# Small input features token by token behind the first receptance block, with later softmax pieces, in a hybrid decoder layer on one Trainium2 core

## The chip, the cores and the metric

One core of one Trainium2 chip runs the whole layer. The metric is the device time of one execution in microseconds; the time of a kernel is the median of its runs. TensorE (PE) multiplies, VectorE (DVE) and ScalarE (ACT) do the element-wise work, GpSimd (POOL) very little, and SyncE (SP) issues nearly all DMAs.

## The reference, cut to what matters

A decoder layer of width 2048 over 256 tokens: two parallel token mixers (mLSTM and RWKV-7), cross-attention into 256 memory tokens, and a gated feed-forward. The change touches the narrow columns of the input projection and the softmax of the cross-attention.

```python
proj = h @ w_in                      # h = rms_norm(x)
q, k, v, o, ir, fr = split_cols(mlstm_p, MLSTM_COLS)      # ir, fr: 4 gate columns each
rp = rwkv_p + (shift_right(rwkv_p, 1) - rwkv_p) * mu      # mix with the token before
r, kr, vr, wl, al, gl = split_cols(rp, RWKV_COLS)         # wl, al 64 columns each, gl 160
...
scores = jnp.einsum('bshd,bmhd->bhsm', q, k).astype(jnp.float32) * (XATTN_HEAD_DIM ** -0.5)
p = jax.nn.softmax(scores, axis=-1).astype(v.dtype)
o = jnp.einsum('bhsm,bmhd->bshd', p, v).reshape(B, S, XATTN_WIDTH)
```

`wl`, `al`, `gl`, `ir` and `fr` are 64 + 64 + 160 + 4 + 4 = 296 columns, the small features.

## The kernel before, in words

Every large product is done with three float32r products: activations and weights are each split into a high and a low part (`hh`, `hl` and `wh`, `wl`), and high x high, low x high and high x low are summed in PSUM. The work is a list of blocks, one for 512 output columns as a rule (`block`, run in order by `run`). A block reads its weights in chunks of two k-tiles of 128 rows. `Feed` brings a chunk by a DMA from SP, casts it to `wh` on ACT (L375) and subtracts `wl` on DVE (L396), three chunks ahead of PE in four buffers, so a cast waits until PE has left the chunk four places before. A block is feature-major (`fm`: the weights are stationary, 256 tokens move, the output has features on partitions) or token-major (`tm`: the activations are stationary, the weight columns move, the output has tokens on partitions). Its sums stand in two of four PSUM banks, so a block's first matmul waits until the banks of the block before the last are evacuated.

The rest, evacuations and all other mathematics, is written as Python generators. The planner `Spread` places one piece of them (up to the next `yield`) at a time between the matmuls: at every half chunk (`half`, twice a chunk) DVE gets 640 and ACT 820 units of credit, capped at 1200, and a piece of the first bulk task or of the first two back tasks runs while both credits are positive; chain tasks run every so many halves. `need` runs a task to its end at once. The order on every engine is thus fixed when the program is written.

The order of the blocks at the front: the small features (`sm`, the 296 columns padded to 384, feature-major), receptance 0 and 1 (`r_evac`), keys, values, and so on. While the first block runs, the input is split (`x_split`), and its squares are summed for the norm (`st0`). `sm_evac` ends the statistic (`st0.finish`: a fold on DVE, a column matmul, the root on POOL, a row matmul, a copy), multiplies the sums by it, mixes each token with the one before (`shiftmix`, ACT then DVE), and adds two tasks: `gates` (mLSTM gates) and `sm_rest` (the low-rank decay and rate, products `zwa`). The keys' groups (`k_group`), `inverses` and the recurrence `rwkv` wait for these, and its end feeds `hb_split` (products `zg`), whose output `hb` a later block needs (`need_hb`).

In the cross-attention the blocks are keys (`xk`), a quarter of the values (`xv`), queries (`xq_`), the rest of the values. Beside them the residual (`Residual.run`) produces the queries' input and the squares of its norm, whose column (`early_column`, tile `st` from `stx`) the softmax needs. `stagger` runs the four heads of `softmax` in steps of one half: scores `xsc`, exponentials `spr`, turned rows `xpT`. The attention product `xo` follows the values.

Of the kernel before, what the change touches and what calls it, by code (L numbers as in the profile page):

```python
# [15 lines left out]
P = 128  # L16
D = 2048
S = 256
# [127 lines left out]
def _layer(ctx, tc, nc, d, dbg):  # L146
# [96 lines left out]
    class Stat:  # L243
# [65 lines left out]
        def early_column(self):  # L309
            self.fold()  # L310
            yield
            yield
            self.column()
# [16 lines left out]
    class Feed:  # L330
        def __init__(self, order):
            self.kind = [k for k, s in order]
            self.src = [s for k, s in order]
            self.raw, self.st, self.nd, self.ns, self.nl = {}, {}, 0, 0, 0

            self.sm = [big(f"wsm{i}", [P, 4, 2, 384]) for i in range(2)]

# [21 lines left out]
        def staged(self, name, r, i):  # L359


            k, c = r.shape[1:]
            up = i - len(self.src) + 384
            o = 0
            if self.kind[i] == "fm":
                o = 16 if i % (16 if up >= 0 else 4) else 24
            w = wp.tile([P, 1024 + 128], F32R, tag=name, bufs=4, name=name)
            return w[:, o:o + k * c].rearrange("p (k c) -> p k c", k=k)

# [39 lines left out]
    def tm_products(o, t, c, wx, first, last):  # L409
        wh, wl, xh, xl = wx  # L410
        t = slice(t // P * P, t // P * P + P)
        c = slice(c, c + 512)
# [19 lines left out]
    def run():  # L432
# [8 lines left out]
        for b, c0, c1 in order:  # L441
            if c0 == 0:
                if len(pend) >= 2 and b["pool"] is acc:
                    side.need(pend[-2])
                if b["before"]:
                    b["before"]()
                n = (b["cols"] // P + 1) // 2 if b["kind"] == "fm" else 2 * (b["cols"] // 512)
                b["banks"], b["k"] = [], 0
                for _ in range(n):
                    if b["pool"] is acc:  # L450
                        if len(ring) >= 4:
                            side.need(ring[-4]["task"])
                        ring.append(b)
                    b["banks"].append(b["pool"](b["kind"], [P, 2, S] if b["kind"] == "fm" or b is xv else None))
                if b["bankwise"]:
# [8 lines left out]
            for ci, s in enumerate(srcs):  # L464
# [9 lines left out]
                for kj in range(s.shape[1]):  # L474
# [19 lines left out]
                    else:  # L494
                        for g, o in enumerate(banks):
                            tm_products(o, g * P * 512 // b["cols"], g * 512 % b["cols"], (wh[:, kj], wl[:, kj], xh, xl),
                                        first, last)
# [46 lines left out]
            if end:  # L544
                b["task"] = side.add(b["evac"](banks))
                if b is xq_:
                    side.need(b["task"])
                pend.append(b["task"])
# [18 lines left out]

    def pre_sm(ci, feed):
        if ci == 0:
# [13 lines left out]

    def pre_r0(ci, feed):
        if ci == 0:
# [17 lines left out]

    def sm_evac(ps):
        dve.tensor_scalar(om, pcol("mu", 0, 27), -1.0, 1.0, op0=ALU.mult, op1=ALU.add)
# [4 lines left out]
        yield from st0.finish(3)  # L610
        pr = PR()
        dve.tensor_mul(pr, ps[0], bc(st0.rb, 2))
        wa, gl = C("wa", "m0"), T2("gl")
# [3 lines left out]
        yield  # L617
        pr = PR()
        dve.tensor_mul(pr[:, 0], ps[1][:, 0], st0.rb)
        shiftmix(gl1, pr[:, 0], 26, slice(0, 32))  # L620
        R = [T2("rows") for _ in range(4)]
        M["rows"] = R
        tasks["gates"] = side.add(gates(), chain=1)
        act.copy(R[0][0:4, 0], pr[32:36, 0])
        act.copy(R[0][0:4, 1], pr[64:68, 0])
        act.activation(wa[0:64], wa[0:64], AF.Tanh)
# [940 lines left out]
    def stagger(gens):  # L1567
# [16 lines left out]
    def softmax(h):  # L1584
# [43 lines left out]

    block("fm", W("w_xk", 0), mxs, kx_evac, before=start_res1)
    xv = block("tm", W("w_xv", 0), mxs, vx_evac, tail=2)  # L1630
# [237 lines left out]
def prepare(i):  # L1868
# [32 lines left out]
    o["con"] = constants()  # L1901
    z = lambda n: np.zeros((D, n), np.float32)
    smw = np.concatenate([w[:, 6152:6440], w[:, 3072:3076], z(28), w[:, 3076:3080], z(60)], 1)
    o["w_sm"] = np.ascontiguousarray(smw.reshape(8, 2, P, 384).transpose(0, 2, 1, 3))
    ga, gb = w[:, 6440:8488], w[:, 8488:10536]
# [29 lines left out]
```

## Time and profile before

| | |
|---|---|
| median of 3 runs | 1896.22 us (1896.04 to 1896.8) |
| profiled execution | 1896.41 us, span 1894.2 us |
| PE busy | 1878.4 us (99% of the span) |
| DVE busy | 1297.0 us (68%) |
| ACT busy | 1012.7 us (53%) |
| mean granted TensorE clock | 0.999 |
| weight DMAs of the small features | 7 of 384 KB and 2 of 192 KB |

Busy time of PE counts overlapping matmuls once; what one of them costs is seen from the starts of its neighbours. A row of a timeline gives start, duration, engine, source line, operation, output and inputs, shape, count, and in brackets the idle time ahead of it with what ended it. In the view of waits a row gives total time, number and longest.

### The profile page before, as it was taken

The numbers are of one execution on the slowest core, as the hardware profiler recorded it, in microseconds if no ns is written. First come the engines' busy times: TensorE is split into PE (matmuls) and PEld (weight loads), VectorE is DVE, ScalarE is ACT, GpSimd is POOL, SyncE is SP. The second block draws the span as 40 slices with busy tenths as digits, with TensorE's granted clock in tenths as the row PEclk, the third lists the DMA queues.
The fourth block names the chain that finished last, engine by engine and source line by source line (L and its number), as shares of the span: only waits on it lengthen the run. The fifth ranks groups of instructions, "written<-read, shape, count | busy, mean of one in ns | idle before, by whom it ended". The sixth has DMA issues, their size and how long they took to land.

```text
span 1894.2 us, 36440 instructions
## 1 busy us (share of the span) xinstructions
PE 1878.4 (99%) x15066; PEld 1788.5 (94%) x15066; DVE 1297.0 (68%) x1834; ACT 1012.7 (53%) x1467; POOL 22.4 (1%) x39
## 2 busy tenths in 40 slices
PE   9999999999999999899999999999999999999998
PEld 9999988999999999899999999999999998888886
DVE  7878787565675857677767766667766675556555
ACT  7676435555454645566555444455444455455554
POOL 0100000000000000000000000000000000000000
PEclk9999999999999999999999999999999999999999
DMA  7655554444556755455555555555566556556554
GB/s 267 184 168 182 183 157 149 136 153 157 167 171 210 268 201 179 134 163 186 193 189 190 191 198 193 197 190 190 191 198 196 195 190 219 192 190 198 191 191 142
DMA packets 98199, 352.20 MB, mean 186 GB/s; under 512 B 11057, under 2 KB 11825, under 8 KB 97649
## 3 DMA queue, kind: packets, MB, share of 16 engines
q1 hardware_dynamic: 97168, 348.86, 56.1%
q8 instruction: 118, 1.93, 0.4%
q10 hardware_dynamic: 864, 1.01, 0.2%
q14 instruction: 49, 0.39, 0.1%
HBM read 347.73 MB, written 2.10 MB: 185 GB/s over the span
## 4 chain that ended last, share of the span: by engine, by line
PE 95%; DVE 2%; ACT 1%; issue 1%; DMA 0%; ACTq 0%; DVEq 0%
PE fm L181 67%; PE tm L181 24%; DVE wl L396 1%; PE gram L181 0%; PE Y L181 0%; ACT wh L375 0%; DVE rows L66 0%; PE lv L181 0%; PE num L181 0%; DMA wsm<-in_w_sm_dram 0%; ACT spr L66 0%; PE X L181 0%; PE gramA L181 0%; PE U L181 0%; DVE ql L66 0%
## 5 line engine op out<-in xcount | busy, mean ns | idle before, releaser
L396 DVE TENSOR_TENSOR wl<-raw,wh 128x1024 fp32r<-128x1024 f32 x640 | 780.1, 1224 | 437.9 <-ACT wh L375 435.1
L375 ACT CAST wh<-raw 128x1024 fp32r<-128x1024 f32 x640 | 668.4, 1049 | 530.5 <-PE fm L181 408.6
L181 PE MATMUL fm<-fh,wh 128*128 128x256 f32 x2048 | 567.4, 277 | 1.4 <-ACT fh L66 1.4
L181 PE MATMUL fm<-fh,wl 128*128 128x256 f32 x2048 | 566.5, 277 | 0.0
L181 PE MATMUL fm<-fl,wh 128*128 128x256 f32 x2048 | 566.4, 277 | 0.0
L181 PEld LDWEIGHTS fm<-fh,wh 128*128 128x128 f32 x2048 | 384.9, 188 | 1.5 <-ACT fh L66 1.5
L181 PEld LDWEIGHTS fm<-fh,wl 128*128 128x128 f32 x2048 | 384.9, 188 | 0.0
L181 PEld LDWEIGHTS fm<-fl,wh 128*128 128x128 f32 x2048 | 384.9, 188 | 0.0
L181 PE MATMUL tm<-wh,as 128*128 128x512 f32 x1024 | 315.7, 390 | 0.8 <-DVE as L66 0.8
L181 PE MATMUL fm<-hh,wh 128*128 128x256 f32 x1072 | 301.9, 282 | 0.0
L181 PE MATMUL fm<-hh,wl 128*128 128x256 f32 x1072 | 299.7, 280 | 0.5 <-DVE wl L396 0.5
L181 PE MATMUL fm<-hl,wh 128*128 128x256 f32 x1072 | 299.3, 279 | 0.0
L181 PEld LDWEIGHTS tm<-wh,as 128*128 128x128 f32 x1024 | 192.2, 188 | 41.1 <-DVE as L66 1.1
L181 PEld LDWEIGHTS fm<-hh,wh 128*128 128x128 f32 x1072 | 202.8, 189 | 1.6 <-ACT hh L66 0.3
L181 PEld LDWEIGHTS fm<-hh,wl 128*128 128x128 f32 x1072 | 202.3, 189 | 1.2 <-DVE wl L396 0.9
L181 PEld LDWEIGHTS fm<-hl,wh 128*128 128x128 f32 x1072 | 202.3, 189 | 0.1
L181 PE MATMUL tm<-wl,as 128*128 128x512 f32 x512 | 199.3, 389 | 0.0
L181 PEld LDWEIGHTS tm<-wl,as 128*128 128x128 f32 x512 | 96.1, 188 | 19.9
L66 ACT CAST as<-ac 128x256 fp32r<-128x256 f32 x128 | 45.6, 405 | 110.8 <-PE tm L181 110.8
L66 DVE TENSOR_TENSOR as<-ac,as 128x256 fp32r<-128x256 f32 x128 | 48.6, 422 | 61.6 <-ACT as L66 61.6
L181 PE MATMUL fm<-mgh,wh 128*128 128x256 f32 x256 | 71.4, 279 | 0.0
L181 PE MATMUL fm<-mgl,wh 128*128 128x256 f32 x256 | 71.2, 278 | 0.0
(376 smaller groups left out, 2168.4 us busy)
## 6 DMA issues: line engine op xcount, KB each, us to landing
raw<-in_w_fu_dram SPq DMA_DIRECT2D x256, 512.0 KB, 4.3
raw<-in_w_in_dram SPq DMA_DIRECT2D x160, 512.0 KB, 3.7
raw<-in_w_fd_dram SPq DMA_DIRECT2D x128, 512.0 KB, 4.3
raw<-in_w_br_dram SPq DMA_DIRECT2D x32, 512.0 KB, 4.2
raw<-in_w_mo_dram SPq DMA_DIRECT2D x32, 512.0 KB, 4.3
raw<-in_w_xk_dram SPq DMA_DIRECT2D x8, 512.0 KB, 4.3
raw<-in_w_xv_dram SPq DMA_DIRECT2D x8, 512.0 KB, 3.7
raw<-in_w_xq_dram SPq DMA_DIRECT2D x8, 512.0 KB, 3.8
```

What stands on the lines that cost most here:

```text
L66: return f(out, *a, **k)
L181: pe.matmul(out, lhsT, rhs, start=start, stop=stop, skip_group_check=True)
L375: nc.scalar.copy(wh, r)
L396: nc.vector.tensor_sub(wl, r, self.st[self.nl][0])
```

## The change

The first receptance block becomes the first block of the list, and its evacuation now begins with the statistic (`statistic`). The small features follow as a token-major block of 296 columns without padding. Their evacuation scales each token by its own factor on ACT, from PSUM to two tiles, waits three halves, turns them with six transposes on PE, and then mixes from PSUM as before. Second receptance block and the rest follow as they were. The keys of the cross-attention are evacuated as soon as their block ends; the statistic column waits five halves instead of two behind its fold; a softmax head is started at every second half, with one half more between scores and exponentials and two more between exponentials and turning. The first eight chunks go into tiles of 512 columns, and the staged weights' rows are padded to a multiple of 64.

```diff
         def early_column(self):
             self.fold()
-            yield
-            yield
+            for _ in range(5):
+                yield
             self.column()
...
-            self.sm = [big(f"wsm{i}", [P, 4, 2, 384]) for i in range(2)]
+            self.sm = [big(f"w0{i}", [P, 4, 2, 512]) for i in range(2)]
...
-            return w[:, o:o + k * c].rearrange("p (k c) -> p k c", k=k)
+            e = -(-c // 64) * 64
+            return w[:, o:o + k * e].rearrange("p (k c) -> p k c", k=k)[:, :, 0:c]
...
-                if b is xq_:
+                if b is xq_ or b is xk:
                     side.need(b["task"])
...
-    def sm_evac(ps):
+    def statistic():
         dve.tensor_scalar(om, pcol("mu", 0, 27), -1.0, 1.0, op0=ALU.mult, op1=ALU.add)
         dve.tensor_scalar(oka, pcol("ka", 0, 8), -1.0, 1.0, op0=ALU.mult, op1=ALU.add)
         for c in (6, 7):
             st0.add(xq[c])
             yield
         yield from st0.finish(3)
-        pr = PR()
-        dve.tensor_mul(pr, ps[0], bc(st0.rb, 2))
+
+    def sm_evac(ps):
+        s1, s2 = T2("smw"), C("smr", "mt1", [P, 2, 96])
+        pool.memset(s2, 0.0)
+        for t in range(2):
+            r = st0.rc[:, t:t + 1]
+            act.activation(s1[:, t], ps[t][:, 0:256], AF.Copy, scale=r)
+            act.activation(s2[:, t, 0:36], ps[t][:, 256:292], AF.Copy, scale=r)
+            act.activation(s2[:, t, 64:68], ps[t][:, 292:296], AF.Copy, scale=r)
+        for _ in range(3):
+            yield
+        pr, p2 = aux("smT", [P, 2, S]), aux("smT", [P, S])
+        for j in range(2):
+            for t in range(2):
+                pe.transpose(pr[:, j, t * P:(t + 1) * P], s1[:, t, j * P:(j + 1) * P], ident)
+        for t in range(2):
+            pe.transpose(p2[0:96, t * P:(t + 1) * P], s2[:, t], ident)
         wa, gl = C("wa", "m0"), T2("gl")
         gl0, gl1 = gl[:, 0], gl[:, 1]
         shiftmix(wa, pr[:, 0], 24)
         shiftmix(gl0, pr[:, 1], 25)
         yield
-        pr = PR()
-        dve.tensor_mul(pr[:, 0], ps[1][:, 0], st0.rb)
-        shiftmix(gl1, pr[:, 0], 26, slice(0, 32))
+        shiftmix(gl1, p2, 26, slice(0, 32))
...
             if hf == 0:
+                yield from statistic()
                 M["rr"] = U("rr")
...
-    block("fm", [d["w_sm"][c] for c in range(8)], xs0, sm_evac, cols=384, pre=pre_sm)
-    for hf in range(2):
-        block("fm", W("w_in", hf), xs0, r_evac(hf), pre=pre_r0 if hf == 0 else None)
+    block("fm", W("w_in", 0), xs0, r_evac(0), pre=pre_r0)
+    block("tm", [d["w_sm"][c] for c in range(8)], xs0, sm_evac, cols=296, pre=pre_sm)
+    block("fm", W("w_in", 1), xs0, r_evac(1))
...
+        n = 1
         while live or left:
-            if left:
+            if left and n % 2 == 0:
                 live.append(left.pop(0))
+            n += 1
...
         dve.tensor_reduce(mx, q, axis=AX.X, op=ALU.max)
         yield
+        yield
...
-        yield
+        for _ in range(3):
+            yield
         q = aux("xpT", [P, 2, S])
```

More of the change, by code (lines that the diff above doesn't have):

```diff
@@ L411, in tm_products @@
         t = slice(t // P * P, t // P * P + P)
-        c = slice(c, c + 512)
+        c = slice(c, c + o.shape[1])
         mm(o, xh[:, t], wh[:, c], start=first, stop=False)
@@ L446, in run @@
                     b["before"]()
-                n = (b["cols"] // P + 1) // 2 if b["kind"] == "fm" else 2 * (b["cols"] // 512)
+                n = (b["cols"] // P + 1) // 2 if b["kind"] == "fm" else 2 * max(1, b["cols"] // 512)
                 b["banks"], b["k"] = [], 0
@@ L453, in run @@
                         ring.append(b)
-                    b["banks"].append(b["pool"](b["kind"], [P, 2, S] if b["kind"] == "fm" or b is xv else None))
+                    o = b["pool"](b["kind"], [P, 2, S] if b["kind"] == "fm" or b is xv else None)
+                    b["banks"].append(o[:, 0:b["cols"]] if b["cols"] < 512 else o)
                 if b["bankwise"]:
@@ L495, in run @@
                         for g, o in enumerate(banks):
-                            tm_products(o, g * P * 512 // b["cols"], g * 512 % b["cols"], (wh[:, kj], wl[:, kj], xh, xl),
+                            n = o.shape[1]
+                            tm_products(o, g * P * n // b["cols"], g * n % b["cols"], (wh[:, kj], wl[:, kj], xh, xl),
                                         first, last)
@@ L566, in x_load, with pre_r0 @@
         sp.dma_start(xq[c], d["x"][:, c * 2:c * 2 + 2])
-    def pre_sm(ci, feed):
+    def pre_r0(ci, feed):
         if ci == 0:
@@ L582, in pre_sm @@
             sp.dma_start(con, d["con"])
-    def pre_r0(ci, feed):
+    def pre_sm(ci, feed):
         if ci == 0:
@@ L623, in sm_evac @@
         tasks["gates"] = side.add(gates(), chain=1)
-        act.copy(R[0][0:4, 0], pr[32:36, 0])
-        act.copy(R[0][0:4, 1], pr[64:68, 0])
+        act.copy(R[0][0:4, 0], p2[32:36])
+        act.copy(R[0][0:4, 1], p2[64:68])
         act.activation(wa[0:64], wa[0:64], AF.Tanh)
@@ L1627, in xo @@
             yield
-    block("fm", W("w_xk", 0), mxs, kx_evac, before=start_res1)
+    xk = block("fm", W("w_xk", 0), mxs, kx_evac, before=start_res1)
     xv = block("tm", W("w_xv", 0), mxs, vx_evac, tail=2)
@@ L1901, in prepare @@
     o["con"] = constants()
-    z = lambda n: np.zeros((D, n), np.float32)
-    smw = np.concatenate([w[:, 6152:6440], w[:, 3072:3076], z(28), w[:, 3076:3080], z(60)], 1)
-    o["w_sm"] = np.ascontiguousarray(smw.reshape(8, 2, P, 384).transpose(0, 2, 1, 3))
+    smw = np.concatenate([w[:, 6152:6440], w[:, 3072:3080]], 1)
+    o["w_sm"] = np.ascontiguousarray(smw.reshape(8, 2, P, 296).transpose(0, 2, 1, 3))
     ga, gb = w[:, 6440:8488], w[:, 8488:10536]
```

## The prediction

> **What bounds the kernel now.** I read the page first: the busy shares of the span (1894.2 us), and the shares of the chain that ended last.
>
> ```profile
> PE 1878.4 (99%) x15066; PEld 1788.5 (94%) x15066; DVE 1297.0 (68%) x1834; ACT 1012.7 (53%) x1467; POOL 22.4 (1%) x39
> ...
> PE 95%; DVE 2%; ACT 1%; issue 1%; DMA 0%; ACTq 0%; DVEq 0%
> ```
>
> TensorE (PE) sets the time nearly everywhere: a change gains only by taking instructions off PE or by removing one of its few waits. The view of waits, kept to PE, begins with these (total us, times, longest):
>
> ```profile
> PE xpT L1611 <- DVE spr L66: 2.7, 4, 1.0
> PE st L181 <- DVE stx L66: 2.3, 1, 2.3
> PE fm L181 <- DVE kT L66: 1.6, 1, 1.6
> ```
>
> All three lie in cross-attention: turning the softmax rows, the statistic column, and the first query matmul, which waits for the banks of the keys. They are 6.6 us, and three of the four later edits are aimed at them. The timeline of PE gives the price of a product as the distance between starts, since matmuls overlap. First the feature-major form (256 moving columns), 32 instructions from the first row to the last; then the token-major form of the cross-attention values (also 256), 8 instructions apart:
>
> ```profile
> 741.05 0.28 PE L181 MATMUL fm<-mh,wh 128*128 128x256 f32 x1
> ...
> 744.68 0.28 PE L181 MATMUL fm<-mh,wl 128*128 128x256 f32 x1
> 799.77 0.28 PE L181 MATMUL tm<-wh,mh 128*128 128x256 f32 x1
> ...
> 800.74 0.28 PE L181 MATMUL tm<-wl,mh 128*128 128x256 f32 x1
> ```
>
> That is 3.63/32 = 0.1134 us and 0.97/8 = 0.121 us.
>
> **The change part by part.** *Small features.* Before: 3 column groups x 16 k x 3 products = 144 instructions x 0.1134 = 16.3 us. After: 2 token halves x 16 x 3 = 96 of 296 columns. No row has 296. The feature-major price scaled by columns gives 0.131, the token-major one scaled gives 0.140; the same form with 40 more columns at 0.1134/256 each gives 0.139, which I take, being nearest in form. 96 x 0.139 = 13.3 us: gain 3.0 us (2.9 to 3.7). [...]
>
> *Turning.* Six transposes are new. The row of the third softmax head is four of them, and the row behind it shows when PE goes on:
>
> ```profile
> 790.12 0.63 PE L1611 MATMUL xpT<-con,spr 128*128 128x128 f32 x4 [1.02 <-DVE spr L66]
> 790.50 0.36 PE L181 MATMUL tm<-wh,mh 128*128 128x256 f32 x1
> ```
>
> 0.38/4 = 0.095 us each, so 0.57 us, and some 0.2 us for entering and leaving (the wait of 1.02 comes ahead of a gap of 1.30): 0.8 us lost (0.6 to 1.0).
>
> *The first block.* It now reads 512 columns per chunk instead of 384, so its first weights are a third larger. The timeline of the start:
>
> ```profile
> 4.80 0.36 DVE L382 CAST wh<-wsm 128x384 fp32r<-128x384 f32 x1 [4.80 <-DMA wsm<-in_w_sm_dram]
> ...
> 6.65 0.51 ACT L386 CAST wh<-wsm 128x384 fp32r<-128x384 f32 x1 [1.52 <-DMA wsm<-in_w_sm_dram]
> ...
> 9.74 0.39 PE L181 MATMUL fm<-hh,wl 128*128 128x256 f32 x1 [0.50 <-DVE wl L396]
> ```
>
> The second half lands 1.85 us after the first, so a third more bytes may cost up to 0.6 us on each of two halves: 1.2 us lost at most if nothing covers it. Against that, a chunk gives PE 24 instructions (2.7 us) instead of 18 (2.0 us), which may swallow the 0.5 us wait for low parts. I take 0.6 us lost, between 0.4 gained and 1.2 lost. After that PE has more cover than now, because preparing a chunk grows less:
>
> ```profile
> L396 DVE TENSOR_TENSOR wl<-raw,wh 128x1024 fp32r<-128x1024 f32 x640 | 780.1, 1224 | 437.9 <-ACT wh L375 435.1
> ...
> L396 DVE TENSOR_TENSOR wl<-wsm,wh 128x768 fp32r<-128x768 f32 x7 | 6.7, 959 | 0.2 <-ACT wh L375 0.2
> ```
>
> *The statistic and the receptance evacuation, now under a block of 13.3 us.* The halves (planner steps) shrink from 1.36 to 0.83 us while the pieces stay. Their chain before:
>
> ```profile
> 35.71 0.61 PE L181 MATMUL stb<-con,st_c 128*128 128x128 f32 x4
> 36.35 0.42 DVE L66 COPY st_b<-stb 128x256 f32<-128x256 f32 x1 [1.06 <-PE stb L181]
> ...
> 38.01 0.69 DVE L66 TENSOR_TENSOR pr<-fm,st_b 128x512 f32<-128x512 f32 x1
> ...
> 40.08 0.42 DVE L66 TENSOR_TENSOR pr<-fm,st_b 128x256 f32<-128x256 f32 x1
> ```
>
> By the planner the row matmul stands at the ninth half, 6.6 us into the block (7.1 with the column matmul ahead of it); copy 0.64 us later; then on DVE the low part of a small chunk (0.78 us, the two rows above extended to 592 columns), the first multiply, the shift-mix of two column groups (ACT and DVE in turn, about 2 us as between 38.01 and 40.08), one full low part (1.22), the second multiply (0.69). The banks come free 13.5 us after the block's start; PE wants them at 13.3 plus 0.7 for the two statistic matmuls, so 14.0. The cover is half a microsecond. The next weights, for the second chunk behind, come about as close. I take 0.4 us lost (0 to 1.5), and 0.3 us (0 to 0.8) for PE reaching the transposes at the fourth half, while ACT does six evacuations queued behind a cast. The memset on POOL and the removed multiplies (0.69 and 0.42 on DVE) lie beside PE.
>
> *What is pushed back.* The gates and the low-rank task are added at half 37 instead of 27. Following the planner's own rule piece by piece (640 and 820 units per half, cap 1200, costs from the lengths in the code), the gates end at half 68 instead of 55, but the low-rank task at 74 instead of 72, the last key group at 142 instead of 141, and the inverses at 195 in both: the credits stood at their cap while tasks waited for each other, and that takes up the delay. One multiply of the queries slips to the handover of its banks, perhaps 0.2 us, inside the 0.4. That this counting holds is seen in two places of the timelines: the inverses' last step in the third half of its block, and the last two gating products at the very start of the block that needs them:
>
> ```profile
> 297.02 1.24 DVE L66 STREAM_TRANSPOSE cmt<-Lt 128x1024 f32<-128x1024 f32 x1
> ...
> 541.76 0.39 PE L181 MATMUL zg<-gs,gwh 128*128 128x256 f32 x2
> ...
> 543.67 0.41 PE L181 MATMUL fm<-hb,wh 128*128 128x256 f32 x2
> ```
>
> I cost it at nothing.
>
> *Keys at once.* Forced at the end of their block, the two multiplies go behind the low part that follows 745.30 instead of to 751.43:
>
> ```profile
> 745.30 2.35 DVE L396 TENSOR_TENSOR wl<-raw,wh 128x1024 fp32r<-128x1024 f32 x2
> ...
> 751.43 1.29 DVE L66 TENSOR_TENSOR kT<-fm,stm_b 128x512 f32<-128x512 f32 x2
> ```
>
> Done by 747.8, wanted by PE at 750.5: the wait of 1.6 us goes (1.3 to 1.6). Behind them on DVE the residual pieces move 1.3 us later and lose two halves of credit, and the value block's low parts with them; the idle time of DVE ahead of the queries' low parts covers it, 2.39 us in the first row below.
>
> ```profile
> 756.24 1.23 DVE L396 TENSOR_TENSOR wl<-raw,wh 128x1024 fp32r<-128x1024 f32 x1 [2.39 <-ACT wh L375]
> 772.74 0.61 PE L181 MATMUL st<-ones,stx 128*128 128x1 f32 x4 [2.29 <-DVE stx L66]
> ```
>
> *Statistic column three halves later.* The fold is ready at 772.7 by the second row, so at 771.1 once the keys' 1.6 us are gone; PE, there at 770.4 now, comes at 770.4 - 1.6 + 3 x 1.36 = 772.9. The wait of 2.3 us goes (1.0 to 2.3). The column lands in the first half of the value chunks behind the queries; the softmax still finds it done.
>
> *Softmax.* A head now starts every second half, its exponentials two halves behind its scores, its turning three halves (over 4 us) behind those: all of the 2.7 us goes. The last head is then turned in the twenty-eighth half, behind the last value matmul, where PE goes into the attention product:
>
> ```profile
> 803.74 3.62 PE L181 MATMUL xo<-pT,xv 128*128 128x256 f32 x16
> 807.00 0.47 PE L181 MATMUL fm<-oT,wh 128*128 128x256 f32 x1
> ```
>
> These sixteen take PE 3.3 us, and the first two heads' products cover the copy of the last one's rows; I take 0.3 us lost (0 to 1.5).
>
> The other edits (row stride of 320 in the staged weights, renamed tiles) issue nothing new.
>
> **Sum.** 3.0 - 0.8 - 0.6 - 0.4 - 0.3 in front = +0.9; 1.6 + 2.3 + 2.7 - 0.3 behind = +6.3; together 7.2 us. The profiled execution took 1896.41 us (its span and 2.2 around it), 0.2 above the median of 1896.22: 1889.2 against its own time, 1889.0 against the median. I say 1889.1 us.
>
> **Rivals.**
> (a) *The short block does not hide its chain.* If each turn between ACT and DVE takes a microsecond more, the banks come free at 16 us and PE waits 2 there and 1.5 for the next chunks: 1889.1 + 3.5 = 1892.6. For: the cover is 0.5 us. Against: DVE has under 12 us of work in it.
> (b) *The softmax's wait moves to its end.* Turning, copy and value evacuation of the last head stand between the last value matmul and the attention product, and the column waits again: 2 + 1.3 lost, 1892.4. For: four heads fill exactly the halves that there are. Against: the first two heads need nothing of the last.
> (c) *Slower: the gating products come too late.* The last two are forced already (541.76 to 543.67). If the recurrence ends over six halves later, both weight splits and four evacuations stand in a row ahead of the first matmul on hb, some 8 to 10 us of PE idle: 1897 to 1899. It decides only if the ten halves are not absorbed before the inverses; the counting says they are.
> (d) *The narrow product is no cheaper.* At 0.17 us per 296 columns the 96 cost what the 144 did: 1892.1. Against: 0.121 at 256.
>
> **Chances.** Forecast 0.66 (own range 1887.0 to 1891.2), (a) 0.12, (b) 0.12, (c) 0.05, (d) 0.05. 0.2% is 3.8 us, about what a measurement of this kernel can tell from no change; faster ends at 1892.4. The forecast, (d) and half of (a) and (b) lie below it: 0.82; the other half and a little of (c): 0.13; slower 0.05. The range takes in (a), (b) and (d), and below the sum the cheap ends (0.7 for the narrow product, 1.0 at the start, 0.9 at the handover and the transposes): 1886.6 to 1893.2.
>
> **What would show it.** Right: the three waits quoted are gone from PE's list or under 0.3 us each; tm with 296 columns starts every 0.13 to 0.14 us; PE goes from the small block into the second receptance block with under 1 us lost; the first matmul on hb starts at about 543.67 - 0.9 = 542.8. Wrong: a wait of over 1 us of fm for pr, or of the transposes for ACT, near 43 us; xo preceded by a gap; zg spread over more than 4 us ahead of hb.

## The result and the profile after

| | before | after |
|---|---|---|
| median, same chip | 1896.51 us (4 runs, 1896.04 to 1897.26) | 1884.55 us (4 runs, 1884.32 to 1885.29) |
| profiled execution, span | 1896.41 us, 1894.2 us | 1884.58 us, 1882.5 us |

The ratio is 0.9934 with a 95% interval of 0.9919 to 0.9949: 12.0 us faster by the medians, 11.8 by the profiled executions, where 7.2 had been forecast. The page of the changed kernel, busy time and shares of the chain:

```profile
PE 1872.3 (99%) x15024; PEld 1783.9 (95%) x15024; DVE 1293.9 (69%) x1832; ACT 1016.4 (54%) x1477; POOL 21.3 (1%) x40
...
PE 97%; DVE 1%; ACT 1%; DMA 0%; issue 0%; ACTq 0%; DVEq 0%
```

PE has 42 instructions less: 48 products fewer and six transposes more. Its list of waits has lost the three rows with which it began before; what is left lies at the start, in the feed-forward and at the end, apart from two of 0.3 us each (`qk`, and one of the two for `wl`, at 72.60):

```profile
PE fm L181 <- ACT fh L66: 1.4, 1, 1.4
PE warm L181 <- POOL ones L210: 1.1, 1, 1.1
PE fm L181 <- DVE wl L397: 1.0, 2, 0.7
PE sum L181 <- ACT diag L66: 0.9, 1, 0.9
PE tm L181 <- DVE as L66: 0.8, 1, 0.8
PE tm L181 <- DVE qk L66: 0.3, 1, 0.3
```

To see where the time went I divided both timelines of PE at the same products: the first product of all, the first of the second receptance block, the first on `hb`, the first of the cross-attention (`mh`), and the first of the feed-forward (`fh`). Lengths in us:

| stage | before | after | difference |
|---|---|---|---|
| start to first product | 5.31 | 5.17 | -0.1 |
| first product to second receptance block | 42.14 | 38.34 | -3.8 |
| from there to `hb` | 496.2 | 496.1 | -0.1 |
| `hb` to `mh` | 177.8 | 177.8 | 0.0 |
| `mh` to `fh` (cross-attention) | 111.9 | 103.9 | -7.9 |
| `fh` to the end | 1060.9 | 1061.2 | +0.3 |

So the front gained 4.1 us in place of 0.9, the cross-attention 7.9 in place of 6.3, and nothing else moved.

Rows of the front, first of the kernel before (its first product, the first receptance product, the first of the second receptance block):

```profile
5.31 0.55 PE L181 MATMUL fm<-hh,wh 128*128 128x256 f32 x1
...
24.05 0.28 PE L181 MATMUL fm<-hh,wh 128*128 128x256 f32 x1
...
47.45 0.28 PE L181 MATMUL fm<-hh,wh 128*128 128x256 f32 x1
```

and of the changed kernel, where the first receptance block comes first and the small block of 296 columns second:

```profile
5.17 0.55 PE L181 MATMUL fm<-hh,wh 128*128 128x256 f32 x1
...
29.56 0.30 PE L181 MATMUL tm<-wh,hh 128*128 128x296 f32 x1
...
33.51 0.30 PE L181 MATMUL tm<-wl,hh 128*128 128x296 f32 x1
33.64 0.50 PE L181 MATMUL st<-ones,st 128*128 128x1 f32 x4
34.01 0.38 PE L181 MATMUL tm<-wh,hh 128*128 128x296 f32 x1
...
43.37 0.30 PE L181 MATMUL tm<-wl,hh 128*128 128x296 f32 x1
43.51 0.28 PE L181 MATMUL fm<-hh,wh 128*128 128x256 f32 x1
...
47.65 0.28 PE L181 MATMUL fm<-hh,wl 128*128 128x256 f32 x1
47.76 0.60 PE L628 MATMUL smT<-con,smw 128*128 128x128 f32 x4
48.20 0.38 PE L630 MATMUL smT<-con,smr 128*96 128x128 f32 x2
48.34 0.37 PE L181 MATMUL fm<-hh,wh 128*128 128x256 f32 x1
```

The thirty products from 29.56 to 33.64 took 4.08 us, 0.136 each. The 0.14 from 43.37 to 43.51 say that the second receptance block found its banks and weights ready. The row of 48.34 carries no bracket either: the transposes took 0.58 us and waited for nobody.

The cross-attention before: the last value product ahead of the queries and the first query product, the last product ahead of the statistic column (whose own row, at 772.74, stands in the prediction), and the last product ahead of the third head's turning (its row too, at 790.12, stands there):

```profile
750.43 0.28 PE L181 MATMUL tm<-wl,mh 128*128 128x256 f32 x1
752.26 0.36 PE L181 MATMUL fm<-qh,wh 128*128 128x256 f32 x1 [1.55 <-DVE kT L66]
...
770.17 0.28 PE L181 MATMUL fm<-qh,wl 128*128 128x256 f32 x1
...
788.82 0.28 PE L181 MATMUL tm<-wl,mh 128*128 128x256 f32 x1
```

and the same places after, with the last head and the attention product:

```profile
746.36 0.28 PE L181 MATMUL tm<-wl,mh 128*128 128x256 f32 x1
746.47 0.28 PE L181 MATMUL fm<-qh,wh 128*128 128x256 f32 x1
...
768.60 0.28 PE L181 MATMUL fm<-qh,wl 128*128 128x256 f32 x1
768.72 0.50 PE L181 MATMUL st<-ones,stx 128*128 128x1 f32 x4
...
787.70 0.28 PE L181 MATMUL tm<-wl,mh 128*128 128x256 f32 x1
787.82 0.60 PE L1632 MATMUL xpT<-con,spr 128*128 128x128 f32 x4
...
791.11 0.60 PE L1632 MATMUL xpT<-con,spr 128*128 128x128 f32 x4
791.55 3.62 PE L181 MATMUL xo<-pT,xv 128*128 128x256 f32 x16
794.82 0.47 PE L181 MATMUL fm<-oT,wh 128*128 128x256 f32 x1
```

Each gap is now the plain pitch of 0.12 (the pitch is the distance between the starts of two products that follow each other without a wait). Read from start to start less that pitch, the old ones were 1.7 us (printed wait 1.55), 2.45 (2.29) and 1.2 (1.02), and the four ahead of the turnings 0.59, 0.38, 1.18 and 1.20, together 3.4 where the view of waits gives 2.7. The printed wait is some 0.16 us short each time, and the rows show why: it counts from the end of the row before, which is printed 0.28 us long, while in a stream the next product starts 0.12 us after it.

### The profile page after: what moved, and what is told of

The parts are those of the page before. It is cut to its first block, busy times and chain, and to the rows that moved or that the text cites. A ratio compares the mean times of both kernels' runs of the same rounds, so it can differ in the third digit from the quotient of the medians.

```text
span 1882.5 us, 36361 instructions
## 1 busy us (share of the span) xinstructions
PE 1872.3 (99%) x15024; PEld 1783.9 (95%) x15024; DVE 1293.9 (69%) x1832; ACT 1016.4 (54%) x1477; POOL 21.3 (1%) x40
## 4 chain that ended last, share of the span: by engine, by line
PE 97%; DVE 1%; ACT 1%; DMA 0%; issue 0%; ACTq 0%; DVEq 0%
PE fm L181 68%; PE tm L181 25%; DVE wl L397 1%; PE gram L181 0%; PE Y L181 0%; PE lv L181 0%; PE num L181 0%; ACT wh L376 0%; DMA w<-in_w_in_dram 0%; DVE rows L66 0%; PE X L181 0%; PE gramA L181 0%; PE U L181 0%; PE zg L181 0%; PE zwa L181 0%
## 5 line engine op out<-in xcount | busy, mean ns | idle before, releaser
L397 DVE TENSOR_TENSOR wl<-raw,wh 128x1024 fp32r<-128x1024 f32 (+1 forms) x640 | 776.2, 1217 | 428.9 <-ACT wh L376 424.5
L376 ACT CAST wh<-raw 128x1024 fp32r<-128x1024 f32 (+1 forms) x640 | 664.8, 1043 | 512.8 <-PE fm L181 387.2
L181 PE MATMUL fm<-hh,wh 128*128 128x256 f32 x1024 | 287.7, 281 | 0.0
L181 PE MATMUL fm<-hh,wl 128*128 128x256 f32 x1024 | 285.7, 279 | 1.2 <-DVE wl L397 1.0
L181 PE MATMUL fm<-hl,wh 128*128 128x256 f32 x1024 | 285.3, 279 | 0.0
L181 PEld LDWEIGHTS fm<-hh,wl 128*128 128x128 f32 x1024 | 193.0, 188 | 2.1 <-DVE wl L397 1.4
L181 PEld LDWEIGHTS fm<-hh,wh 128*128 128x128 f32 x1024 | 193.4, 189 | 1.3
L181 PEld LDWEIGHTS fm<-hl,wh 128*128 128x128 f32 x1024 | 193.1, 189 | 0.1
```

The costliest lines, as they stand in the source:

```text
L181: pe.matmul(out, lhsT, rhs, start=start, stop=stop, skip_group_check=True)
L376: nc.scalar.copy(wh, r)
L397: nc.vector.tensor_sub(wl, r, self.st[self.nl][0])
```

## The experiments

Fourteen kernels, on chips where the kernel before ran at medians of 1897.7 to 1898.2; a ratio is to that kernel on the same chip. Single runs of it there spread over 4 us, so for most runs the stages above say more than the ratio. But each stage is read from one profiled execution. The kernel before and the six runs that leave its front alone (xattn_only, keys_only, column_only, softmax_only and the two with filler) took 41.9 to 43.0 us in the first of these columns and 496.2 to 497.3 in the second, so there a difference of under 1 us says little by itself.

| run | median us | ratio (95%) | first product to second receptance block | to `hb` | cross-attention |
|---|---|---|---|---|---|
| front_only | 1895.01 | 0.9982 (0.9973 to 0.9991) | 38.2 | 496.0 | 113.4 |
| form_only | 1895.42 | 0.9985 (0.9976 to 0.9993) | 39.8 | 496.1 | 111.8 |
| order_only | 1909.28 | 1.0056 (1.0042 to 1.0069) | 42.1 | 505.8 | 113.5 |
| order_wait | 1911.73 | 1.0070 (1.0057 to 1.0083) | 42.7 | 506.8 | 114.9 |
| evac_dve | 1894.90 | 0.9984 (0.9975 to 0.9993) | 38.7 | 496.4 | 113.4 |
| wide_tm | 1896.91 | 0.9996 (0.9988 to 1.0005) | 42.1 | 495.2 | 111.9 |
| gates_later | 1898.81 | 1.0000 (0.9991 to 1.0008) | 41.9 | 497.4 | 113.5 |
| xattn_only | 1889.54 | 0.9951 (0.9939 to 0.9964) | 43.0 | 496.2 | 103.9 |
| keys_only | 1896.58 | 0.9992 (0.9983 to 1.0001) | 42.2 | 497.3 | 110.6 |
| column_only | 1893.90 | 0.9978 (0.9969 to 0.9987) | 42.1 | 496.2 | 109.0 |
| softmax_only | 1894.86 | 0.9983 (0.9974 to 0.9992) | 42.5 | 496.9 | 108.6 |
| front_column | 1890.13 | 0.9961 (0.9948 to 0.9973) | 38.7 | 495.9 | 109.0 |
| fill_gap | 1901.75 | 1.0023 (1.0014 to 1.0032) | 42.7 | 496.6 | 117.6 |
| fill_short | 1897.01 | 0.9996 (0.9987 to 1.0005) | 41.9 | 496.7 | 111.9 |

Theory A throughout was that both misses are misses of size: in the cross-attention a gap is worth its length from start to start, in the front the deductions that I made for the short block were not paid. The rivals put the extra gain elsewhere.

### The two halves of the change

front_only has all of the change up to the transposes and the cross-attention of before; xattn_only the three later edits and the front of before.

> The front of the change alone (receptance 0 first, token-major small features behind it); keys, statistic column and softmax as before. Theory A, read from the two traces (distances between the starts of neighbouring matmuls): small block 16.3 to 13.0 us, transposes -0.7, start 0, and 1.5 us because PE no longer waits for the gates' columns (gcol, gbc): faster than before by 4.1 us, 1892.3. Rival B, the sum on record: 0.9 us, 1895.5.

> The cross-attention part alone (keys at once, column five halves behind the fold, softmax in steps of two halves); front as before. Theory A (a wait costs the whole gap between the starts of the matmuls around it, the slow restart included): 7.8 us faster, 1888.6. Rival B, the view of waits less 0.3 at the end: 6.3 us, 1890.1. If gains of front and cross-attention depend on each other, the two runs do not add to 11.9.

The cross-attention's half gave 7.9 us of its stage, as theory A said. The front's half kept its 38.2 us in front of the second receptance block, 3.9 less than before, but the cross-attention took 113.4 us, 1.6 more than before, and this hid part of the gain. The windows of front_only around the gap for the statistic column (columns: window, its length, PE, PEld, DVE, ACT and POOL busy, the granted clock, DMA share, GB/s):

```profile
767.20:769.50 2.30, 0.08 (x1) 0.00 (x0) 2.20 (x5) 0.09 (x1) 0.00 (x0) 1.00 0.58 205
769.50:771.50 2.00, 1.93 (x16) 1.93 (x17) 1.23 (x3) 0.00 (x0) 0.69 (x1) 1.00 0.65 131
771.50:775.00 3.50, 3.50 (x19) 3.50 (x19) 1.23 (x1) 1.05 (x1) 0.00 (x1) 0.51 0.71 232
775.00:777.00 2.00, 2.00 (x14) 1.72 (x13) 0.00 (x0) 1.50 (x3) 0.00 (x0) 1.00 0.85 250
```

and of the kernel before around the same gap:

```profile
770.10:772.70 2.60, 0.35 (x3) 0.14 (x2) 2.50 (x5) 0.35 (x1) 0.00 (x0) 1.00 0.52 189
772.70:776.00 3.30, 3.26 (x27) 3.26 (x28) 1.31 (x3) 1.05 (x1) 0.70 (x1) 1.00 0.76 205
```

The gap is the same; but in front_only, 2 us behind it, the clock granted was 0.51 for 3.5 us, and PE started 19 products instead of some 30. That this comes of the gap needed a test of its own, below.

### Keys, column and softmax one by one

```diff
-                if b is xq_:
+                if b is xq_ or b is xk:              # keys_only
...
-            yield
-            yield
+            for _ in range(5):                       # column_only
+                yield
...
-            if left:
+            if left and n % 2 == 0:                  # softmax_only, with its four later yields
```

> Only the keys are evacuated at the end of their block. Theory A (gap): the gap of 1.83 us between the last value matmul and the first query matmul closes: 1.8 us faster. Rival B (waits): 1.6. Rival C: the time is handed on, and the wait for the statistic column grows by what PE comes earlier: 0, with st waiting over 3.5 us.

> Only the statistic column waits five halves instead of two. Theory A (gap): the gap of 2.57 us ahead of it closes, 2.5 to 2.7 us faster. Rival B (waits): 2.3. Rival C: the column comes later than the softmax wants it, the waits of the turned rows grow by 1 us or more: 1.3 or less.

> The kernel before with the softmax pieces alone changed: the heads start every second half, and three halves instead of one lie between a head's exponentials and its turning. Theory A (what a removed wait is worth is the whole gap from start to start in PE's rows): in the kernel before the four gaps ahead of the turnings are 0.60, 0.39, 1.19 and 1.21 us and 1.75 us of transposes themselves stand at 0.35 to 0.54 each where 0.35 would do, so the cross-attention (first mixed product 721.5 to first feed-forward product 833.3, 111.8 us) becomes 3.2 to 3.6 us shorter and the time 1893.0 against a before of 1896.5. With the keys (1.2 measured alone) and the statistic column (2.8 measured alone) that adds up to the 7.8 measured for the three together. Theory B (the waits as the view of waits prints them, 2.7 less 0.3 for the last head): 2.4 shorter. Theory C (the gap for the keys or the column grows when the softmax is moved): under 2.

In the cross-attention stage they gave 1.25, 2.86 and 3.23 us, 7.3 together, where all three at once gave 7.9. Column and softmax measured above the printed waits (2.3 and 2.7) and near the gap; the keys alone fell 0.5 short of their gap of 1.7, although the row `kT` is gone from that run's waits. Most of that half microsecond can be found in the pitch. From the first product on `mh` to the first query product keys_only took 29.51 us and xattn_only, with the same edit there, 29.10, and neither waits on the way; but 64 products in the second half of the keys' block started every 0.118 us in keys_only and every 0.113 in xattn_only, in the kernel before and in the changed one. What sets the pitch of a product no run here shows.

### Order and form of the small block

order_only moves the block behind the first receptance block and leaves it feature-major with 384 padded columns; form_only leaves it first and makes it token-major with 296 columns.

```diff
-    block("tm", [d["w_sm"][c] for c in range(8)], xs0, sm_evac, cols=296, pre=pre_sm)   # after
+    block("fm", [d["w_sm"][c] for c in range(8)], xs0, sm_evac, cols=384, pre=pre_sm)   # order_only
```

> The kernel before with the small block behind the first receptance block, still feature by feature with 384 padded columns (288 products of 256 columns) and still evacuated by the multiplies of VectorE; cross-attention as before. Theory A (the order is worth something by itself: the gate pieces come later against the matmuls, and the gaps at the transposes of the gate columns, 1.46 us from start to start at 64.27, and at the broadcast, 0.57 us over the pitch at 72.80, shrink to the 0.65 and 0.2 that the changed kernel shows): first product to the first product of block ha 1.0 to 1.5 us shorter than the 379.2 of before. Rival B (all of the 4.1 us that the front gained came from the narrower token-major products, a deduction of mine was too high and the order costs nothing and gives nothing): within 0.4 of 379.2. Rival C (the small block hid the arrival of the first chunks better, the deduction of 0.6 for the start was right): 0.4 to 0.8 longer at the start, read between the first product and the end of the first block.

> The kernel before with the small block token by token (296 columns, then turned) but still the first block, the statistic computed in its evacuation as before; cross-attention as before. Theory A (form and order each give their part): the block's products take 96 times 0.1355 = 13.0 us instead of 16.3, the transposes cost 0.7, but as first block it is now shorter than the arrival of its inputs, and its evacuation, which must wait for the statistic, stands where nothing is ready to cover it, so 0.5 to 2.6 us shorter between the first product and block ha (379.2 before), with a wait for weights at the start or a gap at the transposes in PE's rows that the changed kernel does not have. Rival B (form explains the whole gain of the front): 3.8 to 4.3 shorter. Rival C: the statistic ahead of the transposes is late and costs more than the products save: no shorter than before.

form_only was 2.3 us shorter up to the second receptance block, 1.5 less than the whole. Its first rows show why: with the small block in front, PE came early to the statistic, 0.90 us before its fold was done.

```profile
26.93 0.28 PE L181 MATMUL fm<-hh,wl 128*128 128x256 f32 x1
28.11 0.61 PE L181 MATMUL st<-ones,st 128*128 128x1 f32 x4 [0.90 <-DVE st L66]
```

The remaining half microsecond is its transposes, which here stand ahead of the second receptance block and in the changed kernel behind its first product.

order_only was against all three theories: nothing gained or lost up to the second receptance block, and 9.6 us lost from there to `hb`. Seven of the eight waits for low parts in the next row lie there (the other, 0.60 us at 10.87, is in the first block), and one of 0.69 for a cast:

```profile
PE fm L181 <- DVE wl L397: 5.8, 8, 1.5
```

The longest is at 145.55, where DVE took four element-wise pieces of the chain (`BK`) ahead of the low part that PE needed:

```profile
141.64 2.59 DVE L66 TENSOR_TENSOR BK<-kt 64x512 f32<-64x512 f32 x4
144.27 2.36 DVE L397 TENSOR_TENSOR wl<-raw,wh 128x1024 fp32r<-128x1024 f32 x2
```

Three runs asked what in the form prevents this. evac_dve is front_only with its six scaled copies on DVE instead of ACT; order_wait is order_only with the pause of three halves ahead of the evacuation; wide_tm is front_only with the 384 padded columns, so that the block has its old length.

```diff
-            act.activation(s1[:, t], ps[t][:, 0:256], AF.Copy, scale=r)
+            dve.tensor_scalar(s1[:, t], ps[t][:, 0:256], r, None, op0=ALU.mult)     # evac_dve, and the other two
...
     def sm_evac(ps):
+        for _ in range(3):                                                          # order_wait
+            yield
```

> The small-feature part of the change alone, with the six scaled copies out of the product banks on VectorE instead of ScalarE. Theory A (what spares the front the waits of the order-only run is that the token-major form takes work off VectorE in its evacuation): waits for the weights' low parts come back between 50 and 200 us, and the way from the first product of the second receptance block to block hb is 1 to 9 us longer than the 496.1 of the front alone. Rival B (VectorE has room, the order-only run lost its 9.5 us to the moment at which the chain of pieces starts): within 0.5 of 496.1, and the time that of the front alone, 3.2 below before.

> The order-only kernel (small block behind the first receptance block, feature by feature, 384 padded columns) with three pieces of waiting at the head of the small block's evacuation, as many as the changed kernel has ahead of its transposes. Rival B of the run above (the moment at which the chain of pieces starts decides): the eight waits for the weights' low parts, 5.8 us in all, shrink to under 2, and the way from the second receptance block to block hb falls from 505.8 to between 496 and 500. Theory A (the work on VectorE decides, not its moment): it stays between 504 and 508.

> The small-feature part of the change alone, token by token, but with the 384 padded columns of before (96 products of 384 columns) instead of 296; the copies out of the banks are four instead of six. Theory A (the token-major form, with its pause and its turning after the evacuation, is what makes the order bearable; the width only prices the products): the product starts every 0.170 to 0.176 us, so that the way from the first product to the second receptance block is 3.3 to 3.9 us longer than the 38.2 of the front alone, 41.5 to 42.1, while the way from there to block hb stays at 496 to 497.5. Rival B (the length of the small block against the pieces that are due behind it decides, and the order-only run lost its 9.5 us because its block took 3.3 us more): the way from the second receptance block to block hb is 500 to 506.

evac_dve kept 496.4, so it does not matter on which of the two engines these copies run. order_wait brought the waits for low parts down, as the theory of the moment said, but the time stayed and went to two later links of the same chain:

```profile
PE tm L181 <- DVE qk L66: 2.9, 1, 2.9
...
PE zg L181 <- ACT gwh L66: 2.5, 1, 2.5
...
PE fm L181 <- DVE wl L397: 1.2, 2, 0.7
```

Behind each of these two waits the granted clock was 0.50 for a while (219.0 to 222.4 and 550.1 to 556.9). In the first of these stretches the products of 512 columns started every 0.43 us, against 0.23 just ahead of it, so that nearly half of the time at that clock was lost; with the 8.3 us at that clock that lie ahead of `hb`, this gives an estimate of 4 us of the 506.8. By that estimate the pause without these stretches would have saved some 3 us, and the stage would still be above the 496 to 500 of that theory.

wide_tm had the long block, 42.1 us to the second receptance block, and 495.2 behind it. So it is the token-major form with its own evacuation, and not the narrow width, that makes the place behind the receptance block bearable; the width alone is worth 3.6 us (the small block took 17.55 us here and 13.95 in front_only). Its 96 products cost 0.1735 us each. Which property of the form decides (the scale per token in place of the broadcast row, the operands in PSUM, the way in which the pieces fall) stays open.

### The gates

```diff
-        for _ in range(4):
+        for _ in range(7):
             yield
         ...
         q8 = aux("gcol", [P, 8, 4])
```

and the same ahead of the broadcast `gbc`.

> The kernel before with seven instead of four pieces of waiting ahead of the transposes of the gate columns, and seven instead of four ahead of the gates' broadcast; nothing else changed. Theory A (these two gaps are the part of the front's gain that I had costed at nothing): the gap at the gate columns (1.46 us at 64.27 in the kernel before) falls to 0.7 and the first broadcast's excess (0.57) to 0.2, so block ha starts 1.0 to 1.4 us earlier, and the time is 1.0 to 1.4 lower. Rival B (these gaps have another cause, such as the change of operation itself, or come back at the next steps of the chain): the gaps remain and block ha starts within 0.3 us of before.

Before, the gates' transposes took 1.05 us in two parts, with a wait between; after, 0.59 in one:

```profile
64.48 0.34 PE L729 MATMUL gcol<-con,rows 4*128 4x4 f32 x3
65.03 0.57 PE L729 MATMUL gcol<-con,rows 4*128 4x4 f32 x5 [0.21 <-DVE rows L66]
65.53 0.39 PE L181 MATMUL fm<-hh,wh 128*128 128x256 f32 x1
```

```profile
80.53 0.65 PE L745 MATMUL gcol<-con,rows 4*128 4x4 f32 x8
81.12 0.39 PE L181 MATMUL fm<-hh,wh 128*128 128x256 f32 x1
```

The broadcast behind them went from 1.02 to 0.66 us. gates_later shows the same 0.58 and 0.66, so the gaps closed; but the stage to `hb` was no shorter. It has a wait of 0.41 us for a low part at 56.67, and that is no effect of the edit: keys_only and softmax_only, with the gates of before, have it at the same place (0.39 and 0.33). Its products on the way to `hb` also came at the slower pitch of some 0.118 us more often than in the kernel before, which cost it some 0.7 us. So this run doesn't settle what the gaps are worth; the interval of its ratio reaches 1.7 us to either side.

### The clock behind the gap

front_column is front_only with the later column. fill_gap and fill_short are the kernel before with products of ones ahead of the statistic column, 18 and 6 of them, so that PE has work while it waits.

```diff
             self.fold()
             yield
             yield
+            q = aux("fill", [P, S])
+            for _ in range(6):
+                mm(q, ones.broadcast_to((P, P)), ones.broadcast_to((P, S)))
             self.column()
```

> The small-feature part of the change and the later statistic column together; keys and softmax as before. In the front alone PE stood still for 2.57 us ahead of the statistic column and then ran at a granted clock of 0.62 and 0.52 until 775, which cost 1.6 us on the way from the first query product to the output projection (56.3 us; 54.7 in the kernel before, which had the same gap and no slow stretch). Theory A (the slow stretch comes of the gap): with the column moved the gap is gone, no stretch under 1.00 follows, and that way takes 51.9 us as in the column alone; the time is the front's 4 to 4.8 and the column's 2.8 below before, ratio 0.9958 to 0.9966. Rival B (the slow stretch comes of the order of the front and has nothing to do with the gap): a stretch at half clock stays somewhere between 760 and 800 and that way takes 53.3 to 53.7 us.

> The kernel before with 18 products of ones (256 columns each, into a tile that nobody reads) ahead of the statistic column of the cross-attention's queries, so that PE is busy for about 2.0 of the 2.57 us in which it stood still; the wait itself stays as long. Theory A (half-clock stretches come of the gap): no stretch under 1.00 behind it in the profile, and as the profiled kernels with the gap had the stretch in 3 of 6, the median lies 0 to 1.7 us below that of before on the same chip. Rival B (the gap has nothing to do with it): the stretch is found as often as without the filler, and the median is that of before within 0.5.

> As the run with the filler, but with 6 instead of 18 products of ones: each took 0.363 us there, so that 6 take 2.2 us and fit into the 2.57 us in which PE otherwise stands still ahead of the statistic column. Theory A (the half-clock stretch comes of the gap, and half or more of the runs of before on this chip have it): the way from the first query product to the output projection is 54.5 to 55.2 us without a stretch under 1.00, and the median lies 0.8 to 1.7 below before. Rival B (the stretch has nothing to do with the gap): a stretch at half clock is found behind it again, or the median is that of before within 0.5.

front_column had no stretch under 1.00 and took exactly the 109.0 us of column_only. In fill_gap the filler was far longer than the gap (7.8 us for the 18, or 0.436 each, and not the 0.363 that the expectation of fill_short starts from), so it cost time and settled nothing. fill_short, with 2.6 us, fits, and the gap has gone from PE without the statistic coming earlier:

```profile
768.00:770.60 2.60, 2.60 (x25) 2.60 (x24) 2.60 (x5) 2.60 (x4) 0.00 (x0) 1.00 0.22 57
770.60:773.20 2.60, 2.60 (x15) 2.23 (x14) 2.50 (x5) 0.24 (x1) 0.00 (x0) 1.00 0.51 187
773.20:776.00 2.80, 2.80 (x26) 2.80 (x25) 1.09 (x2) 0.76 (x1) 0.70 (x1) 1.00 0.76 206
```

Its runs lay between 1896.37 and 1897.89 us, those of the kernel before on the same chip between 1896.48 and 1900.58. The fastest are the same; what is missing is the upper part. Of the ten profiles with a gap of 2.2 us or more ahead of the column, five (front_only, order_only, order_wait, gates_later, evac_dve) have a half-clock stretch behind it and five (before, keys_only, softmax_only, form_only, wide_tm) do not; of the six without the gap none has. That the gap is a condition of the stretch is what these runs support. The medians' ratio for fill_short (0.9987 to 1.0005) doesn't exclude one.

The sixteen traces show where the stretch came and where it did not. All changes of the granted clock that a trace records lie whole multiples of 3.4133 us apart (in front_only 761.17, 3.41 and 1116.16 us, which are 223, 1 and 327 times that; in the kernel before 1884.16 us, 552 times, and in the changed one 1873.92, 549 times), and the first lies anywhere between 3.9 and 10.3 us (7.07 in the kernel before, 6.27 in the changed one). So I divided each trace from its first change on into windows of that length. Leaving out the first 12 us and what follows the last product, the clock fell to 0.50 behind exactly the seven windows, of some 8800, in which PE ran no matmul wider than four columns for 1.96 us or more: five hold the gap ahead of the column, two hold the waits of order_wait named above. In all others that time was at most 1.80 (1.55 in the kernel before, 1.36 in the changed one). In front_only the window from 768.09 to 771.50 has 1.96 us of it; in the kernel before the same gap falls across the edge at 771.66, with 1.21 us ahead of it and 1.55 behind (the statistic matmuls counted in), and no stretch follows. In these two traces it was thus the place of the window's edge that told the gap of 2.57 us with the stretch from the one without, and that place differed from execution to execution. Why the clock falls no run here shows.

## Why the prediction was wrong

Direction and mechanism were right, and the three waits went as described; the sum was 4.7 us too small, in these terms.

- *Products of 296 columns*, +3.0: measured 0.136 us in place of 0.139, so 13.0 us and +3.3. The trace is 2% below my estimate from the rows.
- *The first block*, -0.6: the first block lost 2.4 us against 144 x 0.1134 before (18.74 in all) and 2.6 against 192 x 0.1134 after (24.39), so -0.2. The larger first chunk cost little: the wait for low parts grew from 0.50 to 0.68 us (10.45).
- *Handover*, -0.4: 0.14 us from the last small product to the next block, no wait, so nothing fell due and rival (a) fell. The cover was 0.9 us and not half a microsecond: the steps that the prediction lists add up to 13.1 us, not 13.5, and the second multiply ended at 42.63, 13.07 us into the block, where PE came at 43.51.
- *One price for every feature-major product*, 0.1134: the prediction had no term for its change. The second block of the front lost 0.9 us over its products (13.95 against 13.0), where the receptance block as second had lost 1.6 (23.40 against 21.8). These 0.7 are pitch: before, 147 of its starts came 0.118 us apart, after, as first block, 43. It is no free gain in every execution: keys_only, gates_later and fill_gap, with the order of before, ran this block at the fast pitch of 0.113 us for the most part, then waited 0.25 to 0.62 us for the statistic and took 23.5 to 24.0 us.
- *Turning*, -0.8 and -0.3 for waiting: 0.58 us and 0.08 at the product behind it, no wait; so -0.7 and 0.
- *What is pushed back*, 0: the way to `hb` is 496.1 after and 496.2 before although the turning lies in it, so something gave 0.7 us back. Visible are the gates' transposes (0.46) and their broadcast (0.36), less two waits of 0.3 (`wl` at 72.60 and `qk`). The rest, some 0.5, is pitch again: over 0.1134 a product, the feature-major products of this stage that started 0.1155 to 0.1225 us apart cost 6.7 us before and 6.2 after. The counting of halves was right for the ends of the chains (the first product on `hb` came 0.1 from the old distance); it did not look at the small gaps on the way. With identical fronts the stage differs by up to 1.1 us, so these 0.7 are not beyond doubt.
- *Keys, column, softmax*, 1.6 + 2.3 + 2.7: taken from the view of waits. Start to start they are 1.7 + 2.45 + 3.4, and the column's own row fell from 0.47 to 0.36. This is the failed step in the cross-attention, a wait priced by its printed length: 1.1 of the 1.6 us missing there. The tail's 0.3 is the next.
- *The tail*, -0.3: the last head is turned in 0.44 us from its row to the attention product, and that product takes 3.27 to the output projection, against 3.26 before. Nothing lost; rival (b) fell.

In the front the first failed step is the deductions: 0.6, 0.4 and 0.3 us (and 0.3 for the tail behind) were each charged at a middle value, 1.6 together, and 0.2 fell due. The second is that one price stood for all feature-major products, where the faster pitch gave some 1.1 us (0.6 ahead of the second receptance block, 0.5 behind). What sets the pitch stays open, so that gain was luck. The range had the cheap ends: 1886.6 is the sum less 0.7, 1.0 and 0.9. The time lies 2 us below it because the gap lengths, the tail and the pitch were in no bound. Rival (c) fell (hb at 539.59, no late products), and (d) at 0.136.

## What to carry to other kernels

Price the removal of a wait by the distance between the starts of the products on both sides of it, not by the wait that the profile prints: here removing the three waits printed as 6.6 us was worth 7.9. And before a small remainder is explained, compare the pitch of the products on both sides: here it changed by 4% (0.118 for 0.113 us) between executions of the same code. Where several deductions are each "zero if the cover holds", let the measured cover decide them together instead of charging a part of each. And a block that is moved in a planned order brings its evacuation along: order alone cost 9.6 us here, form alone gave 2.3, both together 3.8.

## What the runs showed of the hardware

A stop of PE of 2.2 to 2.6 us ahead of the statistic column was followed in five of the ten profiles that have it by 3.41 us (6.83 in order_wait) at a granted clock of 0.50, beginning up to 2 us after work had gone on; in front_only it cost 1.6 us. The gap ahead of the first query product (1.83 us) and those ahead of the turnings never showed it. In the sixteen traces the changes of the granted clock lie on a grid of 3.4133 us that begins at another moment in each execution (at 7.07 us in the kernel before, at 6.27 in the changed one). Where PE ran no matmul wider than four columns for 1.96 us or more between two neighbouring moments of that grid, the clock fell to 0.50 at the second of them (seven cases); where that time was 1.80 us or less, it did not fall, the first 12 us and what follows the last product left out. Between these two lengths no trace has a case.

The first product behind a stop or behind small matmuls came some 0.08 us later to its successor than the pitch (0.20 for 0.12 at 752.26 in the kernel before), which no list of waits counts. A feature-major product of 256 columns started every 0.113 us in some stretches and every 0.118 to 0.120 in others, in executions of the same code too. A token-major product of 296 columns started every 0.136 us and one of 384 every 0.1735, against 0.120 for 256: an estimate from these three is 0.00042 us a column and 0.013 us besides, within 1%.
